# Load order, casts on GpSimd and held-back transposes in an attention-score kernel whose store queue never empties

## The chip, the cores and the metric

The kernel runs on one core of a Trainium2 chip. The metric is device time in microseconds (us), the median of several executions; these mostly agree within 0.2%. A profile shows one execution. Its span, from the first to the last instruction, is about 1.8 us shorter than the measured time.

## The reference

```python
q, k: float32 of shape (8 batch, 8 heads, 512 seq, 64 dim)
scale = 1.0 / np.sqrt(64)
out = (np.einsum('bhqd,bhkd->bhqk', q, k) * scale).astype(np.float32)   # (8, 8, 512, 512)
```

Inputs are 16.78 MB, the output is 67.11 MB: the kernel mostly writes.

## The kernel before

The work is four units of two batches. A unit has one 2 MB load of k, one of q, casts to bfloat16 (`xb`), transposes on TensorE (`kT`, `qz`), and eight output tiles `o` of 2 MB. A tile takes four PSUM evacuations and one store. Transposes of the next unit are taken in small steps among the evacuations of this one.

```python
raw_pool = ctx.enter_context(tc.tile_pool(name="raw", bufs=3))
bf_pool = ctx.enter_context(tc.tile_pool(name="bf", bufs=5))
# ... (cut: a pool for kT)
out_pool = ctx.enter_context(tc.tile_pool(name="out", bufs=4))
# ... (cut: a PSUM pool for the transposes)
psum_pool = ctx.enter_context(tc.tile_pool(name="psum", bufs=3, space=bass.MemoryType.PSUM))
# ... (cut)
def load_and_cast(v):
    # ... (cut)
    for src in (k_r, q_r):
        xf = raw_pool.tile([P, 2, J * D], f32, name="xf")
        nc.sync.dma_start(out=xf, in_=src[v])
        xb = bf_pool.tile([P, J, 2, D], bf16, name="xb")
        for s in range(2):
            if v == 0 and src is k_r:
                copy = (nc.vector.tensor_copy, nc.scalar.copy)[s]
            else:
                copy = nc.gpsimd.tensor_copy
            # ... (cut: pinned copy of one half)
# ... (cut)
def scores(v, n):
    # ... (cut)
    o = out_pool.tile([P, RO, S], f32, name="o")
    for i in range(0, RO, 2):
        # ... (cut: two matmuls into ps)
        evacuate(o[:, i:i + 2, :], ps)      # ScalarE and VectorE in turn
        yield
    # ... (cut: src is o, flattened)
    nc.sync.dma_start(out=out_r[v, n], in_=src)
# ... (cut)
for v in range(UNITS):
    ahead = transpose(v + 1, *cast[v + 1]) if v + 1 < UNITS else iter(())
    per_step = 3 if v == 0 else 1
    for n in range(N):
        take(ahead, 1)
        for _ in scores(v, n):
            take(ahead, per_step)
    # ... (cut: the steps that are left)
```

All 40 transfers are issued on one queue, in program order. The queue has 5760 packets, 144 to a transfer, and took 97.7% of the time of the 16 DMA engines.

## Time and profile before

| | before |
|---|---|
| time, median of 4 | 204.10 us (203.98 to 204.17) |
| span of the profiled execution | 202.3 us |
| DMA, share of 16 engines | 97.7% |
| VectorE, ScalarE, PE busy | 64%, 51%, 52% |
| last store issued | 184.9 us |

The main lines stand in the prediction. The first two are from the list of waits (engine and line, what it waited for, total us, times, longest), the third from the same list for SyncE's queue, the last from the DMA queues (packets, MB, share).

```profile
ACT o L62 <- DMA out_dram<-o: 50.9, 24, 3.0
...
DVE o L64 <- DMA out_dram<-o: 28.5, 24, 2.0
```

```profile
SPq L192 <- PEq L192: 0.6, 2, 0.4
```

```profile
q14 instruction: 4, 0.03, 0.0%
```

Both evacuating engines wait for stores, so both are ahead of the DMA queue. The SPq line is the closing barrier of the program, where engines wait for each other after the last store has landed (the barrier's instructions begin at 201.50 us, the last landing recorded is at 201.48). The q14 line stands among the DMA queues, with the kind "instruction": 4 packets of 8 KB. Queue 8, of the same kind, has 4 of 16 KB. I call them fetches of instructions.

Each transfer raised its semaphore 16 times (640 increments for 40 transfers), and the page counts 16 DMA engines. I read this as one increment per engine; that is my reading, as the trace does not name the engine. By it the landing on the median and on the last engine can be taken from the recorded times of these increments (no view prints them). In the kernel before, the last store lands at 198.45 us on the median engine and at 201.53 us on the last; the closing part is 202.31 - 201.53 = 0.78 us. All landings and closing parts here are set so that the last record of the trace starts at the end of the span. That record lasts 0.05 us, so on the clock of the other views every landing stands 0.05 us earlier and every closing part is 0.05 us longer, in all runs alike; differences between runs are the same.

### The profile page before, as it was taken

What the parts mean: (1) busy time and instruction counts of PE and PEld (TensorE: products, weight loads), DVE (VectorE), ACT (ScalarE), POOL (GpSimd) and SP (SyncE); (2) the same over time, 40 slices, a digit from 0 to 9 for tenths busy, and PEclk for the clock granted to TensorE, in tenths of its full rate; (3) what the DMA queues carried; (4) which work ended last, traced back from release to release, by engine and by line L of the source; (5) the groups of instructions that cost most, each with busy time, mean ns of one, the idle gap of its engine ahead of it and who ended that gap; (6) DMA issues with size and microseconds to landing.
All of it is one profiled execution on the core that took longest, in us unless ns stands there. A gap on an engine that the chain in (4) does not pass through costs nothing.

```text
span 202.3 us, 1549 instructions
## 1 busy us (share of the span) xinstructions
PE 106.1 (52%) x512; PEld 50.2 (25%) x512; DVE 129.6 (64%) x133; ACT 102.5 (51%) x130; POOL 26.8 (13%) x20
## 2 busy tenths in 40 slices
PE   0045557755854755858575575656564677642000
PEld 0034424432211322423222233223121222210000
DVE  6875669987765686878787788777544455553000
ACT  2254457967654448484756666574833344442000
POOL 1037775756000000000000000000000000000000
PEclk9999999978799699797979787896969655695555
DMA  6999999999999999999999999999999999999991
GB/s 214 428 441 428 424 441 421 424 395 434 437 421 434 432 423 431 434 428 428 437 424 431 431 424 434 434 428 431 434 428 428 431 434 428 428 437 429 416 447 75
DMA packets 5768, 83.99 MB, mean 415 GB/s; under 512 B 640, under 2 KB 640, under 8 KB 640
## 3 DMA queue, kind: packets, MB, share of 16 engines
q1 hardware_dynamic: 5760, 83.89, 97.7%
q8 instruction: 4, 0.07, 0.1%
q14 instruction: 4, 0.03, 0.0%
HBM read 16.78 MB, written 67.11 MB: 415 GB/s over the span
## 4 chain that ended last, share of the span: by engine, by line
DMA 52%; ACT 13%; DVE 13%; PE 10%; issue 2%; ACTq 0%; DVEq 0%; SPq 0%
DMA out_dram<-o 52%; ACT o L62 6%; DVE o L64 5%; PE ps L134 5%; ACT qz L99 4%; DVE qz L89 3%; ACT kT L99 3%; PE tp L120 3%; DVE kT L99 3%; PE tp L111 2%; DVE xb L83 1%; DVE qz L99 1%; ACTq L62 0%; DVEq L64 0%; SPq L140 0%
## 5 line engine op out<-in xcount | busy, mean ns | idle before, releaser
L134 PE MATMUL ps<-kT,qz 128*128 128x512 bf16 x256 | 87.3, 470 | 52.4 <-ACT o L62 43.3
L64 DVE TENSOR_SCALAR o<-ps 128x1024 f32<-128x1024 f32 x64 | 78.2, 1225 | 44.1 <-DMA out_dram<-o 28.5
L62 ACT ACTIVATE o<-ps 128x1024 f32<-128x1024 f32 x64 | 63.5, 1022 | 64.3 <-DMA out_dram<-o 50.9
L134 PEld LDWEIGHTS <-qz 128*128 128x128 bf16 x256 | 28.6, 115 | 98.6 <-issue 87.2
L83 POOL CAST xb<-xf 128x2048 bf16<-128x2048 f32 x14 | 26.1, 1893 | 21.5 <-DMA xf<-in_q_dram 18.1
L99 DVE COPY kT<-tp 64x512 bf16<-64x512 bf16 x32 | 22.0, 687 | 4.3 <-PE tp L111 3.8
L99 DVE COPY qz<-tp 64x512 bf16<-64x512 bf16 x32 | 22.0, 687 | 4.2 <-PE tp L120 3.7
L111 PE MATMUL tp<-identity,xb 128*128 128x128 bf16 x128 | 13.0, 267 | 17.0 <-DVE xb L83 11.1
L99 ACT COPY kT<-tp 64x512 bf16<-64x512 bf16 x32 | 18.5, 578 | 5.0 <-PE tp L111 4.7
L99 ACT COPY qz<-tp 64x512 bf16<-64x512 bf16 x32 | 18.5, 577 | 4.2 <-PE tp L120 3.9
L120 PE MATMUL tp<-identity,xb 128*128 128x128 bf16 x128 | 13.3, 271 | 8.1 <-ACT qz L99 4.9
L111 PEld LDWEIGHTS <-xb 128*128 128x128 bf16 x128 | 11.2, 122 | 21.3 <-ACT xb L83 11.1
L120 PEld LDWEIGHTS <-xb 128*128 128x128 bf16 x128 | 11.5, 123 | 12.6 <-issue 9.7
L89 DVE MEMSET qz<- 64x2048 uint32 x4 | 7.1, 1765 | 2.6 <-issue 1.4
L83 ACT CAST xb<-xf 128x2048 bf16<-128x2048 f32 x1 | 1.9, 1898 | 6.7 <-DMA xf<-in_k_dram 6.7
L83 ACT ACT_TABLE_LOAD x1 | 1.3, 1283 | 0.7 <-PEq L181 0.7
L83 DVE CAST xb<-xf 128x2048 bf16<-128x2048 f32 x1 | 1.2, 1227 | 0.0
masks.py:199 POOL TENSOR_SCALAR_AFFINE_SELECT identity<-identity 128x128 bf16<-128x128 bf16 x1 | 0.3, 292 | 0.1
masks.py:197 POOL MEMSET identity<- 128x128 bf16 x1 | 0.2, 205 | 0.3 <-POOLq L181 0.3
L181 POOL MEMSET const-float32-0.0<- 128x1 f32 x1 | 0.1, 98 | 0.2 <-issue 0.2
L181 POOL MEMSET const-bfloat16-1.0<- 128x1 bf16 x1 | 0.1, 101 | 0.0
L181 POOL MEMSET const-uint8-127<- 128x1 uint8 x1 | 0.1, 101 | 0.0
(1 smaller groups left out, 0.1 us busy)
## 6 DMA issues: line engine op xcount, KB each, us to landing
out_dram<-o SPq DMA_DIRECT2D x32, 2048.0 KB, 16.1
xf<-in_k_dram SPq DMA_DIRECT2D x4, 2048.0 KB, 11.3
xf<-in_q_dram SPq DMA_DIRECT2D x4, 2048.0 KB, 12.3
```

The lines of the kernel that those rows point to most:

```text
L62: pinned(nc.scalar.mul(out=dst, in_=src, mul=scale))
L64: pinned(nc.vector.tensor_scalar(out=dst, in0=src, scalar1=scale, scalar2=None, op0=mybir.AluOpType.mult))
L83: pinned(copy(out=xb[:, :, s, :], in_=xf[:, s].rearrange("p (j d) -> p j d", j=J)))
L89: nc.vector.memset(qz[half(h), :, :, (1 - h) * U:(2 - h) * U], 0.0)
L99: pinned(copy(out=dst(s, h), in_=src[:, h]))
L111: pinned(nc.tensor.transpose(out=tp[:, j, :], identity=identity, in_=kb[:, j0 + j].rearrange("p s d -> p (s d)")))
L120: pinned(nc.tensor.transpose(out=tp[:, i, jj, :], identity=identity, in_=qb[:, RO * jj + i0 + i].rearrange("p s d -> p (s d)")))
L134: pinned(nc.tensor.matmul(out=ps[:, w, :], lhsT=qz[:, i + w, n, :], rhs=kT[:, n].rearrange("d m s j -> d (m s j)"), start=True, stop=True))
L181: nc = _bacc.Bacc("TRN2", target_bir_lowering=False, num_devices=1)
```

## The change

Its intent, as its short description has it: q of the first unit loads fourth instead of second, GpSimd casts everything, the second unit is transposed only when the loads have ended, and the evacuations alternate so that two of the three PSUM buffers always meet the same engine. Two whole memsets also replace four halves.

```diff
-        if n_evac % 2 == 0:
+        if n_evac % 6 in (0, 2, 3):
             pinned(nc.scalar.mul(out=dst, in_=src, mul=scale))
...
-                if v == 0 and src is k_r:
-                    copy = (nc.vector.tensor_copy, nc.scalar.copy)[s]
-                else:
-                    copy = nc.gpsimd.tensor_copy
+            pinned(nc.gpsimd.tensor_copy(out=xb[:, :, s, :],
...
-        for h in range(2):
-            clear(qz, h)
-    cast = [load_and_cast(v) for v in range(UNITS)]
+        nc.vector.memset(qz, 0.0)
+    kb, qb = {}, {}
+    for into, src, v in ((kb, k_r, 0), (kb, k_r, 1), (kb, k_r, 2), (qb, q_r, 0),
+                         (qb, q_r, 1), (qb, q_r, 2), (kb, k_r, 3), (qb, q_r, 3)):
+        into[v] = load_and_cast(src[v])
...
-        per_step = 3 if v == 0 else 1
-        for n in range(N):
-            take(ahead, 1)
+        for n in range(N):
+            per_step = 1 if v else 2 * (n > 2)
+            take(ahead, min(per_step, 1))
             for _ in scores(v, n):
                 take(ahead, per_step)
```

More of the change, by code (lines that the diff above doesn't have):

```diff
@@ L69, in half, with load_and_cast @@
         return slice(h * D, (h + 1) * D)
-    def load_and_cast(v):
-        both = []
-        for src in (k_r, q_r):
-            xf = raw_pool.tile([P, 2, J * D], f32, name="xf")
-            nc.sync.dma_start(out=xf, in_=src[v])
-            xb = bf_pool.tile([P, J, 2, D], bf16, name="xb")
-            for s in range(2):
-                if v == 0 and src is k_r:
-                    copy = (nc.vector.tensor_copy, nc.scalar.copy)[s]
-                else:
-                    copy = nc.gpsimd.tensor_copy
-                pinned(copy(out=xb[:, :, s, :], in_=xf[:, s].rearrange("p (j d) -> p j d", j=J)))
-            both.append(xb)
-        return both
-    def clear(qz, h):
-        nc.vector.memset(qz[half(h), :, :, (1 - h) * U:(2 - h) * U], 0.0)
+    def load_and_cast(src):
+        xf = raw_pool.tile([P, 2, J * D], f32, name="xf")
+        nc.sync.dma_start(out=xf, in_=src)
+        xb = bf_pool.tile([P, J, 2, D], bf16, name="xb")
+        for s in range(2):
+            pinned(nc.gpsimd.tensor_copy(out=xb[:, :, s, :],
+                                         in_=xf[:, s].rearrange("p (j d) -> p j d", j=J)))
+        return xb
     def rearrange(tp, pattern, dst):
@@ L149 @@
     for qz in qzs:
-        for h in range(2):
-            clear(qz, h)
-    cast = [load_and_cast(v) for v in range(UNITS)]
+        nc.vector.memset(qz, 0.0)
[3 more added lines that the diff above has]
+        into[v] = load_and_cast(src[v])
     ts = {}
-    for _ in transpose(0, *cast[0]):
+    for _ in transpose(0, kb[0], qb[0]):
         pass
     for v in range(UNITS):
-        ahead = transpose(v + 1, *cast[v + 1]) if v + 1 < UNITS else iter(())
-        per_step = 3 if v == 0 else 1
+        ahead = transpose(v + 1, kb[v + 1], qb[v + 1]) if v + 1 < UNITS else iter(())
         for n in range(N):
-            take(ahead, 1)
+            per_step = 1 if v else 2 * (n > 2)
+            take(ahead, min(per_step, 1))
             for _ in scores(v, n):
```

## The prediction

> **What bounds the kernel now.** I read the page from the stage picture downwards, because shares of the whole span cannot tell which engine sets the end of a kernel that first loads, then computes, then stores. The first view is the span in 40 slices of about 5.06 us, with the queue's totals under it.
>
> ```profile
> POOL 1037775756000000000000000000000000000000
> DMA  6999999999999999999999999999999999999991
> GB/s 214 428 441 428 424 441 421 424 395 434 437 421 434 432 423 431 434 428 428 437 424 431 431 424 434 434 428 431 434 428 428 431 434 428 428 437 429 416 447 75
> ...
> q1 hardware_dynamic: 5760, 83.89, 97.7%
> ...
> HBM read 16.78 MB, written 67.11 MB: 415 GB/s over the span
> ```
>
> The DMA row is 9 in every slice but the first and the last: transfers are never short of work from 5 us to 197 us. No compute row is. 16.78 MB are read and 67.11 MB written, together 83.89 MB, and the change touches neither. To see the two ends and the handover from loads to stores I then read a table of stretches (columns: busy microseconds of PE, weight loads, DVE, ACT and POOL, granted clock, DMA share, GB/s).
>
> ```profile
> 0.00:2.00 2.00, 0.00 (x0) 0.00 (x0) 0.78 (x1) 1.27 (x1) 0.70 (x6) 1.00 0.54 98
> 2.00:3.00 1.00, 0.00 (x0) 0.00 (x0) 0.99 (x1) 0.01 (x1) 0.00 (x0) 1.00 0.55 131
> ...
> 34.00:40.00 6.00, 3.63 (x33) 2.08 (x32) 5.88 (x9) 5.89 (x10) 4.68 (x3) 1.00 0.99 423
> 40.00:45.00 5.00, 2.54 (x16) 1.57 (x15) 4.25 (x6) 2.80 (x5) 2.78 (x2) 0.75 1.00 393
> ...
> 100.00:150.00 50.00, 31.41 (x157) 14.48 (x156) 37.77 (x40) 31.50 (x41) 0.00 (x0) 0.85 1.01 430
> ...
> 197.00:199.00 2.00, 0.00 (x0) 0.00 (x0) 0.00 (x0) 0.00 (x0) 0.00 (x0) 0.50 0.56 238
> 199.00:200.00 1.00, 0.00 (x0) 0.00 (x0) 0.00 (x0) 0.00 (x0) 0.00 (x0) 0.50 0.15 66
> ```
>
> So the time is a ramp (the queue is at speed from about 3 to 4 us), 83.89 MB at some 430 GB/s = 195 us, and a tail in which a few of the 16 DMA engines finish later than the rest (238, then 66 GB/s) with all compute over. 3.5 + 195 + about 2 lost in the tail + 2 for the end of the program is the span of 202.3; the measured time adds 1.8. Last I asked what the compute engines wait for: ScalarE waits 50.9 us and VectorE 28.5 us in the evacuations for an output buffer, that is for a store to land. The last store is issued at 184.92 us and its queue drains until 200.5: compute is some 15 us ahead at the end.
>
> [...] the 14 GpSimd casts took 1889 to 1894 ns each while VectorE was busy. So I charge nothing for moving a cast to GpSimd beyond its own length.
>
> **The change, part by part.**
>
> *Casts.* Before, the first k tile is cast by VectorE (1227 ns) beside ScalarE (1898 ns); it landed at 8.66 us and was cast by 10.95. After, GpSimd does both halves: 2 x 1.89 = about 3.75 us, done near 12.4, so 1.5 us later. The fourth load, which needs the first of three raw buffers, is issued near 12.45 instead of 11.02. By then the second load has still until about 13.55 and the third until 18.45 (loads land 4.9 us apart), so 6 us of transfers are queued and the queue doesn't run dry. From then on each load is issued about 3.75 us after the landing three loads before, against 4.9 us between landings: the same 17.3, 22.2, 27.1, 32.0 us as before. Cost on the transfers: 0.
>
> *Load order.* q of the first unit lands as fourth, near 8.66 + 3 x 4.9 = 23.4, instead of second at 13.55; GpSimd casts it by 27.1 instead of 17.3. The transposes of the first k are done by then (start 12.4, two rounds of 4.3 us: 21). The four q groups then go 27.1 to 35.7 in two rounds of 4.3 us (before: 19.31 to 27.9).
>
> *Transposes of unit 2 held back* until the fourth output tile. Before, 13 steps of them stood among the evacuations of each of the first output tiles, which came out at 34.3, 40.8 and 48.2 us. After, nothing stands between them. Working it through with 1.02 us per ScalarE and 1.23 us per VectorE evacuation, three PSUM buffers and the new pattern: first tile A, D, A, A from 35.7, done near 38.9; second (D, D, A, D) near 41.4; third (A, A, D, D) near 44.5. The first store is 4.5 us later, the second about level, the third 4 us earlier. The loads, 16.78 MB, keep the queue to about 43 us, so the late first store has some 4 us in hand. Three stores queued by 44.5 feed it to 43 + 3 x 4.9 = 57.7. The five tiles after carry 40 steps at 9 per tile; before, 13 steps took 6.5 to 7.4 us a tile, so 9 take about 5, and the fourth store comes near 50, the fifth near 55, ahead of need (57.7, 62.6). No hole.
>
> *Memset.* Four of 64 x 2048 words at 1765 ns become two over all 128 partitions of twice the length: 4 x 1.77 = 2 x 3.5 = 7.1 us, ending near 8.8, with VectorE free of work until 13. Cost 0.
>
> *PSUM and engine pattern.* The counts stay at 64 and 64 evacuations (78.2 us DVE, 63.5 us ACT). Two of three buffers always meet the same engine, which can shorten some of the waits of PE (43.3 us for ScalarE, 8.8 us for VectorE). None of those is on the path that sets the end: a tile is ready about 3 us after its buffer comes free, and up to three more stores (14.7 us) are queued. A tile with three VectorE evacuations takes up to 3.7 us instead of 3; also hidden.
>
> *Possible gain.* In 40 to 45 us, where last loads, stores and interleaved transposes meet, the rate was 393 instead of 430 GB/s: 5 x 37 = 185 KB, or 0.43 us; the 423 before it adds 42 KB or 0.1 us. The 439 GB/s of the stretch that follows gives 0.1 back. If reads mixed with writes cause it, a sharper handover may return up to 0.4 us. I take 0.1 of it, since slow DMA engines still finish loads while fast ones have begun stores. Sum: 0 + 0 + 0 - 0.1: 204.15 becomes **204.05**, written as 204.0.
>
> **The rivals.** *A hole at the handover.* If the first q arrives later than reckoned, or the pinned order holds the first evacuations back, the first store comes after 43 us and the queue idles. For it: the first store does move to 38.9, close to the end of the loads. Against it: 4 us of margin from two durations measured in this trace. Each further microsecond of delay would cost about one; a likely miss of 2 us costs nothing, of 6 us some 2, giving 206. *GpSimd becomes the bound of the loads.* 16 casts x 1.89 = 30.3 us, serial, with 3.75 us per tile against a load of 4.9[...]. The constant 1893 ns speaks against it[...]. *The intended gain arrives.* Earlier third and fourth tiles and fewer PE waits look like several microseconds on the compute engines, but those wait for stores anyway; whatever they gain turns into a longer wait for an output buffer. For a real gain the transfer rate would have to rise: the 0.4 us above, giving 203.7. *A slower evacuation rhythm* (three in a row on VectorE) would show only if queued stores fell to none, for which no view gives a hint.
>
> **Range and chances.** The centre is 204.0. Three runs of the kernel before spread 0.12 us, so noise is small; the range must hold the handover's 0.4 us, some 0.5 us of luck in how the last DMA engines drain, and a small hole: 203.1 to 205.0. Two per cent is 4.1 us. Faster by that would need a time below 200.1, less than 195 us of transfers plus both ends allow (chance 0.01); slower needs a hole or starved loads of 4 us (0.02); the rest, 0.97, is within 2%.
>
> **What would show it.** In the changed profile: the DMA row still 9 in all but the first and last slice and the total near 97 to 98%; GpSimd with 16 casts of about 1.89 us ending by 49 us; the first store issued near 39 us, the third near 44; the last load issued near 32; ScalarE's and VectorE's waits for stores as long as now or longer; rate in 40 to 50 us at or above 416 GB/s, the mean of 393 and 439. I am wrong if a slice after the first reads below 8 in the DMA row, if casts on GpSimd are longer than 2 us, if loads land more than 5 us apart, or if the steady rate moves from 430 GB/s, which nothing in the change should do.

The forecast's sum, 0 + 0 + 0 - 0.1 us on 204.15, came to 204.05, written as 204.0. The zero for the casts rests on their measured length alone. Two things in it are suppositions of mine: that reads mixed with writes lower the rate, and the 0.5 us of luck at the end. That slow DMA engines still finished loads while others had begun stores can be read off the kernel before: the last load landed at 42.5 us on the median engine and at 45.1 us on the last, and between 42.5 and 45 us the DMA share was 0.99.

## The result, and the profile after

The changed kernel takes 204.72 us (204.60 to 204.87, 4 runs) against 204.10 us. The ratio is 1.0031, with a 95% interval of 1.0014 to 1.0049. Such a ratio is the mean time of one kernel's runs over that of the other's in the same rounds, so it is not quite the ratio of the medians. The change costs about 0.6 us, 0.3%: small, but clear of noise.

First the slices and queues of the changed kernel.

```profile
POOL 1377777711500000000000000000000000000000
...
DMA  6999999999999999999999999999999999999990
GB/s 213 433 433 430 430 433 427 427 414 436 420 433 436 419 431 433 423 433 436 423 430 436 420 433 436 423 436 430 423 436 433 423 436 423 433 430 430 428 420 39
...
q1 hardware_dynamic: 5760, 83.89, 97.4%
...
q14 instruction: 3, 0.02, 0.0%
```

The DMA row is again 9 from the second slice to the last but one: no hole opened where the loads hand over to the stores. GpSimd (POOL) has a gap and a late burst that the kernel before had not. The table of stretches, with the same columns as in the prediction, shows the handover and the ends:

```profile
0.00:2.00 2.00, 0.00 (x0) 0.00 (x0) 0.34 (x1) 1.27 (x1) 0.70 (x6) 1.00 0.57 106
...
40.00:45.00 5.00, 4.23 (x31) 2.18 (x29) 4.30 (x5) 3.35 (x4) 1.55 (x1) 1.00 1.01 416
...
100.00:150.00 50.00, 31.08 (x144) 14.00 (x146) 35.07 (x37) 31.71 (x41) 0.00 (x0) 0.80 1.01 430
...
197.00:199.00 2.00, 0.00 (x0) 0.00 (x0) 0.00 (x0) 0.00 (x0) 0.00 (x0) 0.50 0.48 205
199.00:200.00 1.00, 0.00 (x0) 0.00 (x0) 0.00 (x0) 0.00 (x0) 0.00 (x0) 0.50 0.08 33
```

The steady rate is the same 430 GB/s. The stretch 40 to 45 us moved 416 instead of 393 GB/s, and less is left for the tail (205 and 33 against 238 and 66). By its transfers the changed kernel is not behind: the median DMA engine lands the last store at 198.35 us, 0.10 us before that of the kernel before. So the loss must lie after that. The waits say where part of it is (changed kernel, all engines, then SyncE's queue):

```profile
ACT o L63 <- DMA out_dram<-o: 46.4, 20, 3.9
...
DVE o L65 <- DMA out_dram<-o: 35.1, 19, 3.8
...
POOL xb L78 <- PE tp L102: 8.2, 1, 8.2
```

```profile
SPq L186 <- PEq L186: 0.9, 2, 0.7
```

The sum of the two waits for stores is 81.5 us (before: 79.4), so compute is as far ahead as it was. The SPq line grew from 0.6 to 0.9 us: the closing barrier takes 0.3 us longer. The instruction records name the engine. Before, SyncE, ScalarE, VectorE and TensorE took their last step before the barrier opens at 201.87 to 201.94 us (times of the views, as the next three). After, ScalarE and TensorE came at 202.06 and 202.12, but VectorE only at 202.46. And the last engine landed the last store at 201.71 us instead of 201.53. Together: +0.18 us of last landing, +0.30 us of closing, which is the span's 202.79 - 202.31 = 0.48 us, for this pair of profiles; the medians differ by 0.62. The trace gives the place; the experiments had to say which part of the change puts it there.

### The profile page after: what moved, and what is told of

Read it like the earlier page. It is cut to its first block, busy times and chain, and to the rows that moved or that the text cites. A ratio compares the mean times of both kernels' runs of the same rounds, so it can differ in the third digit from the quotient of the medians. Undisturbed runs are those within 1.5% of the kernel's fastest.

```text
span 202.8 us, 1536 instructions
## 1 busy us (share of the span) xinstructions
PE 103.1 (51%) x503; PEld 49.3 (24%) x512; DVE 126.2 (62%) x130; ACT 100.3 (49%) x129; POOL 30.6 (15%) x22
## 4 chain that ended last, share of the span: by engine, by line
DMA 54%; DVE 11%; PE 11%; ACT 10%; POOL 4%; issue 1%; DVEq 1%; ACTq 0%; SPq 0%
DMA out_dram<-o 44%; DVE o L65 7%; PE ps L125 7%; ACT o L63 7%; DMA xf<-in_q_dram 5%; DMA xf<-in_k_dram 4%; POOL xb L78 4%; PE tp L111 3%; DVE qz L90 3%; ACT qz L90 3%; DVE kT L90 2%; PE tp L102 1%; DVEq L186 1%; ACT kT L90 0%; DVEq L65 0%
## 5 line engine op out<-in xcount | busy, mean ns | idle before, releaser
L125 PE MATMUL ps<-kT,qz 128*128 128x512 bf16 x247 | 83.9, 462 | 51.0 <-ACT o L63 40.2
L65 DVE TENSOR_SCALAR o<-ps 128x1024 f32<-128x1024 f32 x64 | 76.6, 1220 | 41.6 <-DMA out_dram<-o 35.1
L63 ACT ACTIVATE o<-ps 128x1024 f32<-128x1024 f32 x64 | 63.6, 1023 | 55.8 <-DMA out_dram<-o 46.4
L125 PEld LDWEIGHTS <-qz 128*128 128x128 bf16 x256 | 28.0, 113 | 95.2 <-issue 82.7
L78 POOL CAST xb<-xf 128x2048 bf16<-128x2048 f32 x16 | 29.9, 1896 | 22.3 <-DMA xf<-in_k_dram 10.5
L102 PE MATMUL tp<-identity,xb 128*128 128x128 bf16 x128 | 12.4, 260 | 16.1 <-POOL xb L78 12.2
L111 PE MATMUL tp<-identity,xb 128*128 128x128 bf16 x128 | 13.3, 271 | 13.6 <-POOL xb L78 8.5
L141 DVE MEMSET qz<- 128x4096 uint32 x2 | 6.9, 3472 | 2.5 <-PEq L175 1.7
```

The costliest lines, as they stand in the source:

```text
L63: pinned(nc.scalar.mul(out=dst, in_=src, mul=scale))
L65: pinned(nc.vector.tensor_scalar(out=dst, in0=src, scalar1=scale, scalar2=None, op0=mybir.AluOpType.mult))
L78: pinned(nc.gpsimd.tensor_copy(out=xb[:, :, s, :], in_=xf[:, s].rearrange("p (j d) -> p j d", j=J)))
L102: pinned(nc.tensor.transpose(out=tp[:, j, :], identity=identity, in_=kb[:, j0 + j].rearrange("p s d -> p (s d)")))
L111: pinned(nc.tensor.transpose(out=tp[:, i, jj, :], identity=identity, in_=qb[:, RO * jj + i0 + i].rearrange("p s d -> p (s d)")))
L125: pinned(nc.tensor.matmul(out=ps[:, w, :], lhsT=qz[:, i + w, n, :], rhs=kT[:, n].rearrange("d m s j -> d (m s j)"), start=True, stop=True))
```

## The experiments

Two theories. **End only**: no part costs transfer time, and the 0.6 us lie in which DMA engine finishes last and in the closing barrier. Its rivals blame one part: the engine pattern, the handover or the late q, the casts. All kernels gave correct results. A run marked b is an edit of the kernel before, one marked a of the changed kernel. They ran in three groups of four on three chips, each group beside the kernel before, which took 204.07, 204.12 and 204.10 us.

**1. The engine pattern alone (`p_evac`, b).**

```diff
-        if n_evac % 2 == 0:
+        if n_evac % 6 in (0, 2, 3):
```

> The kernel before with the new engine pattern alone. Theory 'end only' (no part costs transfer time; the 0.6 us sit in which DMA engine lands last and in the closing barrier): 203.9 to 204.8, the median DMA engine lands the last store at 198.3 to 198.6 us as before. Rival 'pattern': 204.7, and stores issued later in the steady stage.

Measured: 203.99 us against 204.07 (ratio 0.9995, 0.9983 to 1.0008). Median engine 198.34 us, last landing 201.47, closing 0.78. The pattern costs nothing, and gains nothing.

**2. The held-back transposes alone (`p_late`, b).**

```diff
-        per_step = 3 if v == 0 else 1
         for n in range(N):
-            take(ahead, 1)
+            per_step = 1 if v else 2 * (n > 2)
+            take(ahead, min(per_step, 1))
```

> The kernel before with the transposes of the second unit held back alone. 'End only': 203.9 to 204.8, median engine's last landing 198.3 to 198.6. Rival 'handover': the first stores come at about 33, 36 and 38 us while loads still run, more reads mixed with writes, rate in 35 to 45 us below 400 GB/s, last landing on the median engine 0.3 to 0.6 us later.

Measured: 204.12 us (1.0003, 0.9990 to 1.0017). The first four stores were issued at 32.4, 33.2, 35.6 and 40.9 us instead of 34.3, 40.8, 48.2 and 52.5, so a part of the change moved stores by up to 13 us and the end by nothing. This is what a queue that is never empty looks like.

**3. Load order, casts and memsets without the held-back transposes (`p_load`, a).**

```diff
-        if n_evac % 6 in (0, 2, 3):
+        if n_evac % 2 == 0:
...
-            per_step = 1 if v else 2 * (n > 2)
-            take(ahead, min(per_step, 1))
+        per_step = 3 if v == 0 else 1
+            take(ahead, 1)
```

> The changed kernel with the old engine pattern and the old interleaving, so load order, casts and memsets alone. 'End only': 203.9 to 204.8. Rival 'late q': here the second unit's 13 steps a tile meet a first store near 39 us, so the second store comes near 45 us and the third near 52; if the late q is what costs, this run shows it at least in full: 204.7 or more, and the queue nearly dry around 45 to 50 us.

Measured: 208.62 us (1.0227, 1.0213 to 1.0241), a miss for "end only" as I wrote it, which had no cost here; the rival "late q" had named the nearly dry queue. The rows of its profile:

```profile
DMA  6999999987599999999999999999999999999993
GB/s 222 434 428 434 428 434 422 434 361 311 254 406 456 404 426 428 415 444 412 447 412 434 422 415 441 422 431 425 422 437 412 444 412 434 422 425 437 415 431 155
```

From slice 9 to 11 (about 41 to 57 us) the DMA row falls to 8, 7 and 5. Stores were issued at 41.6, 48.1 and 55.1 us, since 13 transpose steps per tile stand between them, and the queue ran dry. The third store lands on the median engine at 61.39 us; in the kernel before at 57.13, a loss of 4.3 us that is never made up: the last landing is 205.81 instead of 201.53. So the new load order needs the held-back transposes. (This run has the old engine pattern too, which had cost nothing in experiment 1.) The change has two parts that only work together.

**4. How much room the late q has (`a_q5`, `a_q6`, a).** The first q as fifth, and as sixth load.

```diff
-    ... (kb, k_r, 2), (qb, q_r, 0), (qb, q_r, 1), (qb, q_r, 2), (kb, k_r, 3), (qb, q_r, 3)
+    ... (kb, k_r, 2), (kb, k_r, 3), (qb, q_r, 0), (qb, q_r, 1), (qb, q_r, 2), (qb, q_r, 3)   # a_q5
+    ... (kb, k_r, 2), (kb, k_r, 3), (qb, q_r, 1), (qb, q_r, 0), (qb, q_r, 2), (qb, q_r, 3)   # a_q6
```

> The changed kernel with the first q loaded fifth. The first q lands one load (4.9 us) later, so the first store is issued near 42.8 us, when the loads (ended at 42.5 on the median engine) are just over. Theory 'margin of 4 us, then one for one': at most 0.7 us over the changed kernel, 204.7 to 205.4. If there is no margin: 4.9 us more, 209.5.

> The changed kernel with the first q loaded sixth: first store near 47.7 us, 9.8 us later than in the changed kernel of whose delay 4.6 were free. 'Margin, then one for one': 5 us over the changed kernel, 209 to 210.5, with the DMA share low between 43 and 48 us. If stores catch up later (they can't, if the queue is the bound all along): less.

Measured: 206.59 and 211.55 us, against 204.66 for the unaltered changed kernel in the same group: +1.9 and +6.9, both above what was expected. The slices of `a_q6`, and its line on the time from a store's issue to its landing:

```profile
DMA  6999999907999999999999999999999999999993
```

```profile
DMA to landing us min/median/max: 6.3/15.2/17.0
```

The DMA row holds a 0 at about 42 to 47 us: the hole is there, plain. The sizes follow from the landings. The first store was issued at 37.9 us in the changed kernel and landed at 47.34 on the median engine; here it was issued at 43.0 and 48.2 and landed at 49.31 and 54.55, 6.3 us after its issue both times, which is what these stores took that found an empty queue (the shortest in `p_load` took 6.3 us too). The last landing of the whole kernel moved by 203.73 - 201.71 = 2.0 us and 208.95 - 201.71 = 7.2 us, and the first store's landing by 1.97 and 7.21: one for one. (The median engine's last landing moved more, by 3.2 and 8.5 us, while the last engine's lag behind it fell from 3.4 to 2.1 us; why stores followed each other 4.91 us apart there instead of 4.87 stays open.) Of the delays of 5.1 and 10.3 us, 3.1 were free in each. So the room was 3.1 us. Expected were 4.6 for `a_q6` and at least 4.2 for `a_q5`; that reckoning set the issue of the store against the landing of the last load (42.4 us), but the stores issued to an empty queue took 6.3 us to land and the queued ones followed 4.9 us after their predecessors, so 1.4 us of start-up must be taken off: 42.4 + 4.9 - 6.3 = 41.0 us is, by this estimate, the latest issue that costs nothing.

**5. The changed kernel again (`after_again`), and the number of VectorE instructions (`a_memset4`, a; `b_memset2`, b).** VectorE's late step in the closing barrier suggested that the length of its instruction stream matters. The memsets allow a test in both directions.

```diff
-        nc.vector.memset(qz, 0.0)                                                      # a_memset4
+        for h in range(2):
+            nc.vector.memset(qz[half(h), :, :, (1 - h) * U:(2 - h) * U], 0.0)
```

> The changed kernel once more, unaltered, for a second profile. 'End only': 204.6 to 204.9; VectorE again late in the closing barrier by about 0.5 us; the median DMA engine lands the last store near 198.35, the slowest 3.1 to 3.7 us after it. If the slowest engine's lag is chance it may differ from the 3.36 us of the first profile by some tenths.

> The changed kernel with four half memsets as before, two more VectorE instructions, nothing else. In the changed kernel VectorE's step in the closing barrier came 0.5 us after the other engines', which moved the end by 0.3 us. 'End only': if that lateness hangs on where the instruction stream ends, two more instructions may remove it: 204.3 to 204.5; the rest (the slowest DMA engine, 0.2 us later) may stay. If the cost lies in the body: 204.7 unchanged.

> The kernel before with two whole memsets in place of four halves, so two VectorE instructions fewer. 'End only': if the place where VectorE's stream ends decides its lateness in the closing barrier, this run may show it late as the changed kernel does, and 204.4 us; if not, 204.1. Rival (the load order makes the whole 0.6): 204.1 with no lateness.

Measured: 204.66, 204.65 and 204.16 us. `after_again` repeats the closing of 1.08 us and VectorE's lateness. In `a_memset4`, with two more VectorE instructions, the barrier line of SyncE's queue is back to its old size:

```profile
SPq L187 <- PEq L187: 0.6, 2, 0.4
```

and the closing is 0.78 us. But the time did not fall: in this profile the last engine landed at 202.02 us, 0.31 later than in the changed kernel. So the late VectorE step alone does not account for the 0.6 us. `b_memset2` did not become late in the barrier (0.78 us) and stayed at the time of the kernel before.

**6. The remaining combinations (`b_late_evac`, b; `a_order_old`, `a_cast_old`, a).** `b_late_evac` joins the diffs of experiments 1 and 2. The other two undo the load order, or the cast of the first k, in the changed kernel:

```diff
-    for into, src, v in ((kb, k_r, 0), (kb, k_r, 1), (kb, k_r, 2), (qb, q_r, 0), ...    # a_order_old
+    for into, src, v in ((kb, k_r, 0), (qb, q_r, 0), (kb, k_r, 1), (qb, q_r, 1), ...
...
-            pinned(nc.gpsimd.tensor_copy(out=xb[:, :, s, :], ...                         # a_cast_old
+            copy = (nc.vector.tensor_copy, nc.scalar.copy)[s] if first else nc.gpsimd.tensor_copy
+            pinned(copy(out=xb[:, :, s, :], ...
```

> The kernel before with the held-back transposes and the new engine pattern together, old load order and casts. If these two cost nothing together: 203.9 to 204.2, closing part 0.78 us after the last landing. If the 0.6 us come of their combination: 204.6.

> The changed kernel with the old load order (k, q, k, q, ...), GpSimd still casting all. If the order makes the 0.6 us: 203.9 to 204.2. If the casts on GpSimd do: 204.6. If neither, but how the last engine drains: 204.1 to 204.7, with the median engine's last landing at 198.3 to 198.5 and the difference in the slowest engine's lag and the closing part.

> The changed kernel with the first k tile cast by VectorE and ScalarE as before, new load order. If the order makes the 0.6 us: 204.5 to 204.8. If the casts do: 203.9 to 204.2. VectorE has one instruction more, so the closing part may fall to 0.78 us, as it did with two more.

Measured: 204.07, 204.56 and 204.85 us. With the old order the changed kernel is still slow, and with the old cast too, so undoing either alone does not remove the loss (0.5 us of it is left with the old order). No run puts the new order or the casts into the kernel before together with the held-back transposes. All profiles side by side (landings of the last store; times of the first column in us, medians):

| kernel | time | median engine | last engine | closing | q14 fetches of 8 KB |
|---|---|---|---|---|---|
| before | 204.10 | 198.45 | 201.53 | 0.78 | 4 |
| `p_evac` | 203.99 | 198.34 | 201.47 | 0.78 | 4 |
| `p_late` | 204.12 | 198.39 | 201.57 | 0.78 | 4 |
| `b_late_evac` | 204.07 | 198.48 | 201.50 | 0.78 | 4 |
| `b_memset2` | 204.16 | 198.33 | 201.81 | 0.78 | 5 |
| changed | 204.72 | 198.35 | 201.71 | 1.08 | 3 |
| `after_again` | 204.66 | 198.35 | 201.68 | 1.08 | 3 |
| `a_order_old` | 204.56 | 198.43 | 201.71 | 1.08 | 3 |
| `a_memset4` | 204.65 | 198.33 | 202.02 | 0.78 | 4 |
| `a_cast_old` | 204.85 | 198.32 | 202.11 | 0.97 | 4 |

The median engine is within 0.16 us in all ten, in no relation to the time. Everything that differs comes after it. The late closing goes with the instruction fetches: the kernels in which VectorE is late in the barrier (the three with 1.08, and `a_q5` and `a_q6` with 1.10) have three fetches on queue 14 within the span and two right after its end; those where VectorE was in time have four or five. It is tempting to say that VectorE waited there for its own last instructions. But no fetch on record falls into the delay: in the changed kernel the last one before VectorE's late step (202.46 us) began at 189.7 us, and the next two at 203.1. What it waited for stays open. In `a_cast_old` and `p_load`, with four fetches each, ScalarE was the late one.

The last engine's landing is 201.5 to 201.8 us in the first five rows and 201.7 to 202.1 in the others. The two groups overlap, and one profile a kernel is thin: that of `b_memset2` is of a run of 204.36 us, 0.2 above its median. Which part of the change shifts the landing, if one does, I could not settle, since undoing order, cast or memsets one at a time leaves it there.

The increments do show how the lag of the last engine grows. In all ten kernels it jumps, by 0.8 to 1.5 us, in the first transfer whose median landing comes after the first 16 KB fetch of instructions (queue 8) has begun, and this place moves with the fetch: 32 us in the kernel before, 38 with the held-back transposes, 46 in the changed kernel. In the kernel before it went from 0.62 to 1.63 us there, in the changed kernel from 0.32 to 1.63; these two fetches took 1.10 and 1.08 us, where a data packet of 16 KB took 0.61 in the median. It jumps again, by 0.5 to 0.6 us, in the store that the last engine works on during the 8 KB fetches near 186 to 190 us, and by 0.9 us in `a_cast_old`, where two of them began within 0.02 us. In the changed kernel the rest is a slow drift, in steps under 0.2 us. But in the kernel before the lag also went from 1.49 to 2.55 us in the last load, and after the fetch at 32.0 us none is on record before 69.3. No run removes a fetch, so that they cause the jumps is inferred.

**7. A bet on the slow engine (`b_tail120`).** The last store of `b_late_evac` cut into 120 and 8 partitions.

```diff
-        nc.sync.dma_start(out=out_r[v, n], in_=src)
+        cut = 120 if (v, n) == (UNITS - 1, N - 1) else P
+        for rows in (slice(0, cut), slice(cut, P)):
+            if rows.start < P:
+                nc.sync.dma_start(out=out_r[v, n, rows], in_=src[rows])
```

> The run b_late_evac with its last store cut into one of 120 partitions and one of 8. In all profiles so far one DMA engine landed the last store 3.1 to 3.7 us after the median engine, and it sets the end. A bet that it is the engine that gets the last 8 partitions of 128, which is then spared about 4.9 us of work: last landing 199.5 to 200.8 instead of 201.5, time 202.9 to 203.5. If it is another engine, which then may get 0.6 us more: 204.0 to 204.8.

Measured: 206.83 us (1.0130, 1.0116 to 1.0144), a clear miss. Its rate row ends badly:

```profile
DMA  6999999999999999999999999999999999999982
GB/s 208 441 425 435 431 425 438 403 416 431 435 422 444 420 430 428 425 438 422 444 419 441 425 428 431 422 447 416 441 425 438 422 422 447 416 441 422 390 249 80
```

The end ran slowly: 390 and 249 GB/s in the two slices before the last, where the others have about 430, while the DMA row stayed at 9 and 8. From 192 us on many data packets took 1 to 1.9 us, against the usual 0.61. The last landing was at 204.17 us. The edit also did not do what the bet assumed: it presupposed that 8 neighbouring partitions go to one engine, which no trace had shown. The 8-partition store raised its semaphore eight times as data landed, from 198.9 to 204.2 us, which by my reading above is eight engines and not one. The bet lost for another reason than either expected, and says nothing on which engine is slow; why the packets slowed down no run tests. No kernel that I ran beats the kernel before by more than noise.

## Why the prediction was right or wrong

- **Right: what bounds the kernel, and "within 2%".** 204.72 us lies in the range 203.1 to 205.0. The DMA row stayed at 9, the steady rate at 430 GB/s, the last load was issued at 31.7 us (said: near 32), and the waits for stores grew from 79.4 to 81.5 us in sum (ScalarE's alone, which should not have shrunk, went from 50.9 to 46.4). That the time came out inside the range is in part luck: the 0.6 us lie at the end, which the text gave room for but did not reckon.
- **Right: each part costs the transfers nothing.** Shown for the pattern and the held-back transposes alone (experiments 1 and 2), and for the whole by the median engine, 198.35 against 198.45 us. The stores came as worked out: 37.9, 40.8 and 43.8 us, where the text had 38.9, 41.4 and 44.5. The fourth and fifth came at 47.0 and 55.4 (said: 50 and 55).
- **Wrong: the sign.** Forecast was -0.1 us, measured +0.6. The sum "0 + 0 + 0 - 0.1" left out two terms, the last DMA engine's lag and the closing barrier. The text named both ends of the kernel, then held them constant. They measured +0.18 us and +0.30 us in the first pair of profiles. The +0.30 came back in `after_again` and `a_order_old`; the +0.18 is less than the 0.34 us by which the five kernels without the new order differ among themselves (201.47 to 201.81). What sets the 0.6 us stays open: `a_memset4` has the short closing and still took 204.65 us. "A few of the 16 DMA engines finish later" was read off correctly, but allowed for only in the range. Its split of the end, 2 us of tail and 2 of closing, was off too: the last engine lags 3.1 us, and the closing takes 0.8.
- **Not shown: the gain of 0.1 us at the handover.** The stretch 40 to 45 us rose from 393 to 416 GB/s in the first profile, but a second profile of the same kernel has 400, and `b_memset2`, with the old handover, has 413. The figure wanders by as much as the gain. That reads mixed with writes lower the rate was not shown either: with its earlier stores `p_late` moved 405 GB/s in the slice from 40.5 to 45.5 us, the kernel before 395.
- **Too wide: "some 4 us in hand".** The room was 3.1 us (experiment 4). The term left out is the 1.4 us of start-up of a store that finds an empty queue. "Each further microsecond of delay would cost about one" held between `a_q5` and `a_q6`: 5.2 us more of delay moved the last landing by 5.2 and the time by 5.0; "a miss of 6 us some 2" would have been 2.9.
- **Missed: a coupling.** The prediction treated the held-back transposes as a separate part with no cost. Without them the new order costs 4.5 us (experiment 3). The text's own figure of 6.5 to 7.4 us for a tile with 13 steps would have shown it, had the parts been combined.
- **Missed, without harm: a wait on a buffer.** GpSimd's casts were to end by 49 us. The last two began only at 49.7, after a wait of 8.2 us for PE. That the five `xb` buffers were full, because the second unit's k keeps its buffer until its delayed transposes, is my reading of that wait. No load waited for those casts. The durations were right (1896 ns). The two memsets took 3472 ns each (said: 3.5 us) and ended at 9.4 us (said: 8.8), also without harm.
- **Thin: a cast on GpSimd costs only its own length.** The constant 1889 to 1894 ns were read as a sign that VectorE's work beside a cast does not lengthen it. But the one VectorE cast, of the first k at 9.7 us, ended before the first GpSimd cast began at 13.6, and beside the GpSimd casts VectorE only copied and evacuated from PSUM. In the changed kernel the three casts with no VectorE instruction beside them took 1895 to 1897 ns, and one beside a memset for 1.02 us took 1891. Other operations of VectorE no run sets beside a cast.

## What to carry to other kernels

While the store queue was never empty here, reordering compute moved waits and not the end (`p_late` moved stores by up to 13 us and took 204.12 us against 204.07). So ask first whether any store is issued so late that the queue runs dry, and count the start-up of a store that finds it empty (here 6.3 us to land, against 4.9 us between queued stores). Check parts of a change in combination: one may be harmless only because another is there (the new load order cost 4.5 us without the held-back transposes). When two kernels differ by a few tenths of a per cent, compare when the median and the last DMA engine land the last transfer, and the closing barrier, before blaming the body.
